# Gate and up projection: a fourth summed K pair, four low weight parts per product made by an accumulating transfer, and matmuls with the low weight part last

## The chip, the core and the metric

The kernel runs on one core of one Trainium2 chip. The metric is device time in microseconds. TensorE (PE) does the matmuls, VectorE (DVE) and ScalarE (ACT) prepare operands and results, GpSimd (POOL) and SyncE (SP) here mostly issue transfers (DMAs); each has its own queue and works it off in order, and they wait for each other by semaphores.

## The reference

An encoder block on 256 tokens of width 2048: two attentions side by side, a cross attention, then a SwiGLU, each added to the residual, and a final norm. What matters here is the SwiGLU with a hidden width of 5632:

```python
hf = rms_norm(x, g_ffn[layer])
x = x + (jax.nn.silu(hf @ w_gate[layer]) * (hf @ w_up[layer])) @ w_down[layer]
return rms_norm(x, g_final)
```

All inputs are float32.

## The kernel before, in words

Every operand of a matmul is split into a high part `h` (the value rounded to the matmul's format) and a low part `l` (what is left), and a product takes three matmuls: high by high, high by low, low by high (`mm`, L97). The activations are the stationary operand (128x128), the weights the moving one (512 columns). ACT makes `wh` by a cast, DVE makes `wl` by subtracting `wh` from the raw weights (`split_into`, L105).

Weights come as "pairs": 256 rows of K by 1024 output columns, 1 MB, in a tile `wraw` with three buffers, loaded by SP (`pair_raw`, L211). `wh` and `wl` have four buffers each, of 1024 columns. A plain pair ("P") is a two by two block product for two token tiles (tt), two column halves (oc) and two K halves (k): 8 products, 24 matmuls. A summed pair ("W") is done with 7 products of sums of blocks (Strassen's scheme in Winograd's form), 21 matmuls: DVE forms four sums of weight blocks `tsum` (L287 to L292, one instruction of 1024 columns and two of 512), and more parts have to be split. The sums of the activations, `forms`, are made once (`summed_pair`, L237).

`wide_project` (L254) goes through the eight pairs of one product in a given order and accumulates in PSUM; `wide_result` (L325) adds what the summed pairs have left, eight instructions of 512 columns on DVE and one copy on ACT. `wide_chunk` (L901) does this for gate, applies Silu on ACT (L906), does the same for up, multiplies and transposes. There are five chunks of 1024 columns, so ten such products, and behind groups of chunks the down projection (`wide_add`, L342) with pairs of its own. `GU_KINDS` (L39) says which pairs are plain or summed, `G_ORDER` and `U_ORDER` (L41) in which order they come; pair i of either is the same slice of the activations.

The order in which each engine gets its instructions is set by a scheduler when the program is built, from the order of the code, buffers and its own estimate of durations. So instructions of neighbouring pairs are interleaved on every engine, but once built the order is fixed.

Of the kernel before, what the change touches and what calls it, by code (L numbers as in the profile page):

```python
# [35 lines left out]
NFC = FF // 512  # L36
NPC = (FF - 512) // 1024

GU_KINDS = "PPWPWPWP"  # L39

G_ORDER, U_ORDER = (0, 1, 2, 3, 4, 5, 6, 7), (0, 2, 1, 4, 3, 6, 5, 7)  # L41

OUT_KINDS, OUT_ORDERS = ("PPPPWWPP", "PPPPWWWP"), ((0, 1, 2, 3, 4, 6, 5, 7), (0, 1, 2, 4, 3, 5, 7, 6))

# [36 lines left out]
def encoder_block(ctx: ExitStack, tc: tile.TileContext, a, out):  # L81
# [14 lines left out]

    def mm(o, l, r, start, stop, seeded=False):  # L97

        nc.tensor.matmul(o, l.h, r.h, start=start, stop=False, skip_group_check=seeded)  # L99
        nc.tensor.matmul(o, l.h, r.l, start=False, stop=False, skip_group_check=seeded)  # L100
        nc.tensor.matmul(o, l.l, r.h, start=False, stop=stop, skip_group_check=seeded)  # L101

    last_split, last_cast = [None], [None]

# [115 lines left out]
        return Split(*[pool.tile([P, 1024], F32R, name=x, tag=x, bufs=bufs)[:, :n * 512].rearrange(  # L220
            "p (b c) -> p b c", b=n) for x in tags])

    def split_blocks(src, pool=None):
        w = w_tile(src.shape[1], pool)
        split_into(w, src)
        return w

    class Pair:
# [22 lines left out]
        split_into(f[:, 4:8, :], s)  # L251
        return Pair(forms=f)

    def wide_project(pairs, src, order, kinds, leave, join, closed=(0, 1), before=None, seed=None):  # L254
# [10 lines left out]
        for n, i in enumerate(order):  # L265
# [2 lines left out]
                before(n)  # L268
            raw = pair_raw(src[i])
            if i not in summed:  # L270
                w = [split_blocks(raw[:, 2 * k:2 * k + 2, :]) for k in range(2)]
                for tt in range(NT):
                    for oc in range(2):
                        for k in range(2):

                            ends = stop or i == plain[-1] and tt == oc == 1
                            mm(accs[tt][oc], pairs[i].at(k, tt), w[k][:, oc, :], not used[tt][oc],
                               ends and k == 1 and oc in closed, seed is not None)
                            used[tt][oc] = True
                continue  # L280
            if i == summed[0]:
                Q = {q: ps_tile(f"q{q}") for q in (1, 5, 7, 6)}
# [24 lines left out]
            own = i == summed[0], i == summed[-1]  # L307
            t1, t3, t2, t4 = [t[:, j, :] for t in (t13, t24) for j in range(2)] if sum_pool else t13 + t24
            A11, A12, A21, A22, S5, S6, S7, S3 = [pairs[i].forms[:, n, :] for n in range(8)]
            mm(Q[1], A11, b11[:, 0, :], *own)  # L310
            mm(accs[0][1], S3, b11[:, 1, :], False, stop, seed is not None)
            mm(Q[5], S5, t1, *own)
            mm(Q[7], S7, t3, *own)
            mm(accs[0][0], A12, b21[:, 0, :], False, stop, seed is not None)
            mm(Q[6], S6, t2, *own)
            mm(accs[1][0], A22, t4, False, stop, seed is not None)
            if i == summed[-1]:
                leave(Q)
        for tt in range(NT):
# [2 lines left out]
        banks.reverse()  # L322
        return accs

    def wide_result(pairs, src, order, kinds):  # L325
# [12 lines left out]
        def join(tt, oc, acc):  # L338
            r = res[tt][:, oc, :]
            nc.vector.tensor_tensor(out=r, in0=acc, in1=r, op=ALU.subtract if (tt, oc) == (1, 0) else ALU.add)  # L340

        wide_project(pairs, src, order, kinds, leave, join)  # L342
        return res

    def wide_add(pairs, src, order, kinds, oc0, done=None, closed=(0, 1), before=None):
# [554 lines left out]

    def wide_chunk(c, kinds):  # L901

        g = wide_result(xn, a["w_gate"][c], G_ORDER, GU_KINDS)
        for tt in range(NT):
            for oc in range(2):
                nc.scalar.activation(g[tt][:, oc, :], g[tt][:, oc, :], AF.Silu)  # L906
        u = wide_result(xn, a["w_up"][c], U_ORDER, GU_KINDS)
# [182 lines left out]
```

## Time and profile before

| | |
|---|---|
| three runs | 1141.78, 1142.07, 1142.09 us (median 1142.07) |
| the profiled execution | 1141.65 us, of which the span from first to last instruction 1139.8 |
| granted clock of TensorE in it | 0.998 |
| DMA | 222.13 MB, mean 195 GB/s |
| queue of the transfers issued by GpSimd | 3.15 MB |

The page gives each engine's busy time and its share of the span, then the chain of work that ended last, then groups of instructions: line, engine, operation, tiles written and read, shape, count, busy us, mean ns of one, and idle time before them with who ended it. A window's row gives the busy us of each engine, the granted clock, the DMA engines' share and GB/s. A row of the timeline gives the start, the length and what ran, with a count where equal instructions are merged. A row of the waits gives who waited for whom: us in total, times, the longest. A DMA row gives the size and the median time from issue to landing.

### The profile page before, as it was taken

What the parts mean: (1) busy time and instruction counts of PE and PEld (TensorE: products, weight loads), DVE (VectorE), ACT (ScalarE), POOL (GpSimd) and SP (SyncE); (2) the same over time, 40 slices, a digit from 0 to 9 for tenths busy, and PEclk for the clock granted to TensorE, in tenths of its full rate; (3) what the DMA queues carried; (4) which work ended last, traced back from release to release, by engine and by line L of the source; (5) the groups of instructions that cost most, each with busy time, mean ns of one, the idle gap of its engine ahead of it and who ended that gap; (6) DMA issues with size and microseconds to landing.
All of it is one profiled execution on the core that took longest, in us unless ns stands there. A gap on an engine that the chain in (4) does not pass through costs nothing.

```text
span 1139.8 us, 14403 instructions
## 1 busy us (share of the span) xinstructions
PE 1130.6 (99%) x5390; PEld 946.4 (83%) x5390; DVE 973.2 (85%) x1322; ACT 667.5 (59%) x965; POOL 58.6 (5%) x75
## 2 busy tenths in 40 slices
PE   9999999999999999999999999999999999999997
PEld 7888888888788888888888888888888888888886
DVE  7788766878896777989898988998998898999895
ACT  7755455567566555665565555565554564665663
POOL 5910000000001000000000000000000000000000
PEclk9999999999999999999999999999999999999999
DMA  9655333546567444455556556556555555565553
GB/s 362 241 195 185 124 125 139 181 149 224 191 227 259 156 161 179 161 211 189 212 194 219 185 191 218 185 190 216 185 187 220 201 205 190 191 247 196 195 181 129
DMA packets 35494, 222.13 MB, mean 195 GB/s; under 512 B 4321, under 2 KB 5601, under 8 KB 11105
## 3 DMA queue, kind: packets, MB, share of 16 engines
q1 hardware_dynamic: 33696, 216.60, 52.9%
q0 software_dynamic: 864, 3.15, 0.8%
q10 hardware_dynamic: 864, 1.47, 0.4%
q8 instruction: 42, 0.69, 0.2%
q14 instruction: 28, 0.22, 0.1%
HBM read 219.11 MB, written 2.10 MB: 194 GB/s over the span
## 4 chain that ended last, share of the span: by engine, by line
PE 98%; issue 1%; ACT 0%; DVE 0%; POOLq 0%; POOL 0%; ACTq 0%
PE acc L99 26%; PE acc L101 26%; PE acc L100 26%; PE q L100 4%; PE q L99 4%; PE q L101 4%; PE pt L502 2%; PE ppt L650 1%; PE psc L100 1%; PE psc L101 1%; PE psc L99 1%; PE acckv L99 0%; PE acckv L101 0%; PE acckv L100 0%; PE pt L922 0%
## 5 line engine op out<-in xcount | busy, mean ns | idle before, releaser
L107 ACT CAST wh<-wraw 128x1024 fp32r<-128x1024 f32 (+2 forms) x401 | 389.8, 989 | 283.2 <-PE acc L101 219.5
L108 DVE TENSOR_TENSOR wl<-wraw,wh 128x1024 fp32r<-128x1024 f32 (+2 forms) x401 | 455.3, 1148 | 88.8 <-ACT wh L107 86.8
L107 ACT CAST wh<-tsum 128x1024 fp32r<-128x1024 f32 (+1 forms) x98 | 98.0, 1006 | 73.1 <-PE acc L101 29.7
L108 DVE TENSOR_TENSOR wl<-tsum,wh 128x1024 fp32r<-128x1024 f32 (+1 forms) x98 | 113.6, 1165 | 19.5 <-ACT wh L107 19.5
L100 PE MATMUL acc<-wl,x2n_h 128*128 128x512 f32 x320 | 124.5, 390 | 0.0
L101 PE MATMUL acc<-wh,x2n_l 128*128 128x512 f32 x320 | 123.9, 389 | 0.0
L99 PE MATMUL acc<-wh,x2n_h 128*128 128x512 f32 x320 | 108.2, 390 | 0.0
L100 PE MATMUL acc<-wl,x0T_h 128*128 128x512 f32 x224 | 88.5, 395 | 0.0
L101 PE MATMUL acc<-wh,x0T_l 128*128 128x512 f32 x224 | 88.2, 394 | 0.0
L99 PE MATMUL acc<-wh,x0T_h 128*128 128x512 f32 x224 | 86.9, 396 | 0.0
L100 PE MATMUL q<-wl,forms_h 128*128 128x512 f32 x191 | 74.3, 389 | 0.0
L101 PE MATMUL q<-wh,forms_l 128*128 128x512 f32 x191 | 74.1, 389 | 0.0
L100 PE MATMUL acc<-wl,hT_h 128*128 128x512 f32 x188 | 73.3, 392 | 0.0
L101 PE MATMUL acc<-wh,hT_l 128*128 128x512 f32 x188 | 72.4, 389 | 0.0
L101 PEld LDWEIGHTS acc<-wh,x2n_l 128*128 128x128 f32 x320 | 60.1, 188 | 12.4
L100 PEld LDWEIGHTS acc<-wl,x2n_h 128*128 128x128 f32 x320 | 60.1, 188 | 12.3
L99 PEld LDWEIGHTS acc<-wh,x2n_h 128*128 128x128 f32 x320 | 59.9, 188 | 12.3
L99 PE MATMUL q<-wh,forms_h 128*128 128x512 f32 x191 | 66.7, 389 | 0.0
L99 PE MATMUL acc<-wh,hT_h 128*128 128x512 f32 x188 | 64.5, 391 | 0.0
L100 PE MATMUL acc<-wl,forms_h 128*128 128x512 f32 x162 | 62.5, 389 | 0.0
L101 PE MATMUL acc<-wh,forms_l 128*128 128x512 f32 x162 | 62.4, 389 | 0.0
L99 PE MATMUL acc<-wh,forms_h 128*128 128x512 f32 x162 | 61.3, 389 | 0.0
(402 smaller groups left out, 2247.9 us busy)
## 6 DMA issues: line engine op xcount, KB each, us to landing
wraw<-in_w_gate SPq DMA_DIRECT2D x44, 1024.0 KB, 4.8
wraw<-in_w_up SPq DMA_DIRECT2D x44, 1024.0 KB, 4.8
wraw<-in_w_dn SPq DMA_DIRECT2D x41, 1024.0 KB, 4.8
wraw<-in_w_in SPq DMA_DIRECT2D x24, 1024.0 KB, 4.8
wraw<-in_w_out SPq DMA_DIRECT2D x16, 1024.0 KB, 4.8
wraw<-in_w_in_lat SPq DMA_DIRECT2D x5, 832.0 KB, 7.2
wraw<-in_w_xk SPq DMA_DIRECT2D x4, 1024.0 KB, 5.4
wraw<-in_w_xq SPq DMA_DIRECT2D x4, 1024.0 KB, 5.9
```

Of the source, the lines that this page charges most:

```text
L99: nc.tensor.matmul(o, l.h, r.h, start=start, stop=False, skip_group_check=seeded)
L100: nc.tensor.matmul(o, l.h, r.l, start=False, stop=False, skip_group_check=seeded)
L101: nc.tensor.matmul(o, l.l, r.h, start=False, stop=stop, skip_group_check=seeded)
L107: last_cast[0] = nc.scalar.copy(out=dst.h, in_=src).ins
L108: last_split[0] = nc.vector.tensor_tensor(out=dst.l, in0=src, in1=dst.h.bitcast(F32), op=ALU.subtract).ins
L502: nc.tensor.transpose(out=pt[:, j * P:(j + 1) * P], in_=src[:, j * P:(j + 1) * P], identity=ident)
L650: nc.tensor.transpose(out=pt[:, kt * S + tt * P:kt * S + (tt + 1) * P], in_=p[:, tt, kt * P:(kt + 1) * P], identity=ident)
```

## The change

Gate and up get four summed pairs of eight in place of three (pair 7 becomes summed), in new orders. In each product four of the 1024-column low parts of plain pairs are made in another way, those in `G_CARRIED` and `U_CARRIED`, as (pair, K half): ACT writes the negated, rounded weights into `wl`, then casts `wh`, and GpSimd issues a transfer of the raw weights (512 KB, from one on-chip tile to another) that adds to what stands in `wl`. DVE has no part in these. In all products of the kernel the matmul with the weights' low part now comes last, and for plain pairs and some summed products, last of several products. The cores of the diff:

```diff
-GU_KINDS = "PPWPWPWP"
-G_ORDER, U_ORDER = (0, 1, 2, 3, 4, 5, 6, 7), (0, 2, 1, 4, 3, 6, 5, 7)
+GU_KINDS = "PPWPWPWW"
+G_CARRIED, U_CARRIED = {(0, 0), (0, 1), (1, 1), (5, 1)}, {(0, 1), (1, 1), (3, 1), (5, 1)}
+G_ORDER, U_ORDER = (0, 1, 2, 4, 3, 6, 7, 5), (0, 2, 1, 4, 3, 6, 7, 5)
...
     def mm(o, l, r, start, stop, seeded=False):
-        nc.tensor.matmul(o, l.h, r.h, start=start, stop=False, skip_group_check=seeded)
-        nc.tensor.matmul(o, l.h, r.l, start=False, stop=False, skip_group_check=seeded)
-        nc.tensor.matmul(o, l.l, r.h, start=False, stop=stop, skip_group_check=seeded)
+        mm_late([(o, l, r, start, stop)], seeded)
+
+    def mm_late(products, seeded=False):
+        for o, l, r, start, stop in products:
+            nc.tensor.matmul(o, l.h, r.h, start=start, stop=False, skip_group_check=seeded)
+            nc.tensor.matmul(o, l.l, r.h, start=False, stop=False, skip_group_check=seeded)
+        for o, l, r, start, stop in products:
+            nc.tensor.matmul(o, l.h, r.l, start=False, stop=stop, skip_group_check=seeded)
...
-    def split_blocks(src, pool=None):
+    def split_blocks(src, pool=None, by_transfer=False):
         w = w_tile(src.shape[1], pool)
-        split_into(w, src)
+        if by_transfer:
+            nc.scalar.activation(w.l, src, AF.Copy, scale=-1.0)
+            last_cast[0] = nc.scalar.copy(out=w.h, in_=src).ins
+            nc.gpsimd.dma_start(out=w.l, in_=src, accum_op=ALU.add)
+        else:
+            split_into(w, src)
         return w
...
-                w = [split_blocks(raw[:, 2 * k:2 * k + 2, :]) for k in range(2)]
-                for tt in range(NT):
-                    for oc in range(2):
-                        for k in range(2):
+                w = [split_blocks(raw[:, 2 * k:2 * k + 2, :], by_transfer=(i, k) in carried) for k in range(2)]
+                for k in range(2):
+                    products = []
+                    for tt in range(NT):
+                        for oc in range(2):
                             ends = stop or i == plain[-1] and tt == oc == 1
-                            mm(accs[tt][oc], pairs[i].at(k, tt), w[k][:, oc, :], not used[tt][oc],
-                               ends and k == 1 and oc in closed, seed is not None)
+                            products.append((accs[tt][oc], pairs[i].at(k, tt), w[k][:, oc, :], not used[tt][oc],
+                                             ends and k == 1 and oc in closed))
                             used[tt][oc] = True
+                    mm_late(products, seed is not None)
...
-            mm(Q[1], A11, b11[:, 0, :], *own)
-            mm(accs[0][1], S3, b11[:, 1, :], False, stop, seed is not None)
-            mm(Q[5], S5, t1, *own)
-            mm(Q[7], S7, t3, *own)
-            mm(accs[0][0], A12, b21[:, 0, :], False, stop, seed is not None)
-            mm(Q[6], S6, t2, *own)
-            mm(accs[1][0], A22, t4, False, stop, seed is not None)
+            mm_late([(Q[1], A11, b11[:, 0, :], *own), (accs[0][1], S3, b11[:, 1, :], False, stop)], seeded)
+            mm_late([(Q[5], S5, t1, *own), (Q[7], S7, t3, *own)], seeded)
+            mm(accs[0][0], A12, b21[:, 0, :], False, stop, seeded)
+            mm_late([(Q[6], S6, t2, *own), (accs[1][0], A22, t4, False, stop)], seeded)
```

The place that is shown now is pair 1 of the up product of the third chunk; the pair that comes before it in the order is pair 2 (summed), the one behind it pair 4 (summed). On ACT before, `wraw_7026` is pair 1, `wraw_6979` pair 2 and `wraw_7060` pair 4; `wh_7028` and `wh_7032` are the two K halves:

```order
L107 CAST wh2_7001<-tsum_6989 128x1024
L107 CAST wh_6995<-wraw_6979 128x512
L107 CAST wh_7028<-wraw_7026 128x1024
L107 CAST wh_7032<-wraw_7026 128x1024
L906 ACTIVATE res1_6893<-res1_6893 128x512 x2
L107 CAST wh_7062<-wraw_7060 128x1024
```

On ACT in the changed kernel, `wraw_7101` is pair 1, `wraw_7054` pair 2 and `wraw_7136` pair 4; `wl_7108` is the carried low part of pair 1's second half:

```order
L115 CAST wh_7070<-wraw_7054 128x512
L919 ACTIVATE res1_6966<-res1_6966 128x512
L115 CAST wh_7103<-wraw_7101 128x1024
L919 ACTIVATE res1_6966<-res1_6966 128x512
L235 CAST wh_7107<-wraw_7101 128x1024
L115 CAST wh_7138<-wraw_7136 128x1024
L234 ACTIVATE wl_7108<-wraw_7101 128x1024
L115 CAST wh_7144<-tsum_7142 128x1024
```

Between the cast of pair 1's first half and the negated copy now stand one Silu and two casts, one of them of the next pair; the transfer is issued by GpSimd behind the copy.

On PE before, at the same pair, where `wl_7029` and `wl_7033` are the low parts that DVE makes:

```order
L100 MATMUL acc_6944<-wl_7029,x2n_h_4508 128x512
L101 MATMUL acc_6944<-wh_7028,x2n_l_4509 128x512
L99 MATMUL acc_6944<-wh_7032,x2n_h_4508 128x512
L99 MATMUL q1_6981<-wh_7062,forms_h_4531 128x512
L100 MATMUL acc_6941<-wl_7033,x2n_h_4508 128x512
L101 MATMUL acc_6941<-wh_7032,x2n_l_4509 128x512
```

On PE in the changed kernel, from the last matmuls with the second half's high part to the first with its carried low part:

```order
L107 MATMUL acc_7018<-wh_7107,x2n_l_4509 128x512
L106 MATMUL q1_7056<-wh_7138,forms_h_4531 128x512
L107 MATMUL q1_7056<-wh_7138,forms_l_4532 128x512
L109 MATMUL q1_7056<-wl_7139,forms_h_4531 128x512
L106 MATMUL q5_7057<-wh_7144,forms_h_4531 128x512
L107 MATMUL q5_7057<-wh_7144,forms_l_4532 128x512
...
L109 MATMUL q7_7058<-wl_7145,forms_h_4531 128x512
L106 MATMUL q6_7059<-wh2_7154,forms_h_4531 128x512
L107 MATMUL q6_7059<-wh2_7154,forms_l_4532 128x512
L109 MATMUL acc_7015<-wl_7108,x2n_h_4508 128x512
```

Eleven matmuls of the next pair now stand ahead of the carried low part. The matmul that frees the buffer for `wh_7103` (the last one with pair 0's first high part) stands 45 matmuls ahead of the first with `wl_7108`.

More of the change, by code (lines that the diff above doesn't have):

```diff
@@ L252, in summed_pair, with wide_project @@
         return Pair(forms=f)
-    def wide_project(pairs, src, order, kinds, leave, join, closed=(0, 1), before=None, seed=None):
+    def wide_project(pairs, src, order, kinds, leave, join, closed=(0, 1), before=None, seed=None, carried=()):
         accs = [[acc_tile() for _ in range(2)] for _ in range(NT)]
@@ L309, in wide_project @@
             A11, A12, A21, A22, S5, S6, S7, S3 = [pairs[i].forms[:, n, :] for n in range(8)]
-            mm(Q[1], A11, b11[:, 0, :], *own)
-            mm(accs[0][1], S3, b11[:, 1, :], False, stop, seed is not None)
-            mm(Q[5], S5, t1, *own)
-            mm(Q[7], S7, t3, *own)
-            mm(accs[0][0], A12, b21[:, 0, :], False, stop, seed is not None)
-            mm(Q[6], S6, t2, *own)
-            mm(accs[1][0], A22, t4, False, stop, seed is not None)
+            seeded = seed is not None
+            mm_late([(Q[1], A11, b11[:, 0, :], *own), (accs[0][1], S3, b11[:, 1, :], False, stop)], seeded)
+            mm_late([(Q[5], S5, t1, *own), (Q[7], S7, t3, *own)], seeded)
+            mm(accs[0][0], A12, b21[:, 0, :], False, stop, seeded)
+            mm_late([(Q[6], S6, t2, *own), (accs[1][0], A22, t4, False, stop)], seeded)
             if i == summed[-1]:
@@ L323, in wide_project, with wide_result @@
         return accs
-    def wide_result(pairs, src, order, kinds):
+    def wide_result(pairs, src, order, kinds, carried):
         res = []
@@ L340, in join @@
             nc.vector.tensor_tensor(out=r, in0=acc, in1=r, op=ALU.subtract if (tt, oc) == (1, 0) else ALU.add)
-        wide_project(pairs, src, order, kinds, leave, join)
+        wide_project(pairs, src, order, kinds, leave, join, carried=carried)
         return res
@@ L901, in wide_chunk @@
     def wide_chunk(c, kinds):
-        g = wide_result(xn, a["w_gate"][c], G_ORDER, GU_KINDS)
+        g = wide_result(xn, a["w_gate"][c], G_ORDER, GU_KINDS, G_CARRIED)
         for tt in range(NT):
@@ L906, in wide_chunk @@
                 nc.scalar.activation(g[tt][:, oc, :], g[tt][:, oc, :], AF.Silu)
[L907 removed]
+        u = wide_result(xn, a["w_up"][c], U_ORDER, GU_KINDS, U_CARRIED)
         t = act_tile(name="hT")
```

## The prediction

> **What bounds the kernel now.** I read the page's engine totals and its chain first, then the windows of the stage that changes, then the timeline of single instructions there, then waits and DMA landings.
>
> ```profile
> PE 1130.6 (99%) x5390; PEld 946.4 (83%) x5390; DVE 973.2 (85%) x1322; ACT 667.5 (59%) x965; POOL 58.6 (5%) x75
> ...
> PE 98%; issue 1%; ACT 0%; DVE 0%; POOLq 0%; POOL 0%; ACTq 0%
> ```
>
> TensorE is busy in 99% of the span and carries 98% of the chain that ended last. The gate and up stage lies in the next window.
>
> ```profile
> 720.00:820.00 100.00, 100.00 (x451) 82.88 (x449) 92.75 (x119) 61.52 (x79) 0.00 (x0) 1.00 0.56 195
> ```
>
> PE has no gap in these 100 us, at a granted clock of 1.00. DVE is busy for 92.75, ACT for 61.52, the DMA engines for 0.56; GpSimd does nothing. So the time is the number of matmuls times their pitch, as long as nobody makes PE wait.
>
> ```profile
> 639.72 0.39 PE L101 MATMUL acc<-wh,forms_l 128*128 128x512 f32 x1
> ...
> 649.92 0.39 PE L101 MATMUL q<-wh,forms_l 128*128 128x512 f32 x1
> ```
>
> The second of these is the 45th matmul after the first: 10.20 / 45 = 0.2267 us apart. Each ends 0.39 after its start.
>
> ```profile
> ACT wh L107 <- PE acc L101: 249.2, 182, 5.4
> DVE wl L108 <- ACT wh L107: 106.3, 136, 3.6
> ```
>
> ACT waits for PE 182 times: the four buffers each of `wh` and `wl` are full, and a cast starts when matmuls free one. DVE waits for ACT. The helpers run as far ahead as the buffers let them; that lead is what the change spends.
>
> **Part 1: matmuls that go.** A plain pair has 8 products of 3 matmuls, a summed one 7. One pair more is summed in each of 5 x 2 products: 10 x 3 = 30 matmuls (the order has 5360 where the page has 5390). 30 x 0.2267 = 6.8 us, all on the path. This is the most that can be won: PE has no other idle time in this stage.
>
> **Part 2: vector and scalar work.** The pitch of each kind is read from runs of equal instructions.
>
> ```profile
> 619.02 3.50 DVE L108 TENSOR_TENSOR wl<-wraw,wh 128x1024 fp32r<-128x1024 f32 x3
> ...
> 1011.26 1.28 DVE L340 TENSOR_TENSOR res<-acc,res 128x512 f32<-128x512 f32 x2
> ```
>
> ```profile
> 617.94 2.95 ACT L107 CAST wh<-wraw 128x1024 fp32r<-128x1024 f32 x3
> ```
>
> ```profile
> L108 DVE TENSOR_TENSOR wl<-wraw,wh 128x1024 fp32r<-128x1024 f32 x334 | 403.9, 1222 | 78.0 <-ACT wh L107 76.3
> L107 ACT CAST wh<-wraw 128x1024 fp32r<-128x1024 f32 x334 | 345.8, 1052 | 238.1 <-PE acc L101 185.4 <-issue 23.7 <-PE q L101 8.7
> ...
> L340 DVE TENSOR_TENSOR res<-acc,res 128x512 f32<-128x512 f32 x40 | 26.3, 682 | 0.4 <-PE acc L101 0.4
> ...
> L906 ACT ACTIVATE res<-res 128x512 f32<-128x512 f32 x20 | 12.3, 629 | 4.6 <-DVE res L340 4.4
> ```
>
> On DVE 1024 columns cost (3.50 - 1.22) / 2 = 1.14 and 512 cost 1.28 - 0.68 = 0.60. A plain pair is two low parts, 2.28. A summed one is four operations of 1024 (three low parts, one sum) and three of 512: 4 x 1.14 + 3 x 0.60 = 6.36. With 8 operations of 512 for the results, a product had 5 x 2.28 + 3 x 6.36 + 4.8 = 35.3 us on DVE against 183 x 0.2267 = 41.5 on PE. Now it has 4 x 2.28 + 4 x 6.36 + 4.8 - 4 x 1.14 = 34.8 against 180 x 0.2267 = 40.8. The carried low parts pay for the added sums; DVE stays at 85% of PE. On ACT a cast of 1024 has a pitch of (2.95 - 1.05) / 2 = 0.95; a product gains 4 negated copies and the casts of one summed pair instead of a plain one (3 x 0.95 + about 0.6 for the one of 512, less 2 x 0.95), about 5.4 us. ACT was 61.52 of 100, so it goes to some three quarters; no time on the path by itself. A negated copy of 1024 is not in the trace; at 512 columns an ACTIVATE takes 629 ns, so between 0.6 and 1.26 for twice that, and I take the cast's 1.05. The extra summed input pair is formed once, beside gate and up of the first 512 columns: below 3 us of DVE, under PE's matmuls. The other reordering (low weight part last, in the whole kernel) gives DVE more time and takes none from PE; where PE had no gap it can only stay equal or open one. I put it at 0, bounds -0.5 and +1.
>
> **Part 3: the 40 transfers, where the answer lies.** A carried low part goes: buffer free, negated copy on ACT, issue on GpSimd, landing, matmul. PE takes its matmuls in order, so a landing after its place in the order stops PE, everything behind it, and through the buffers ACT and DVE. The tightest place is pair 1, second half, of each up product (the rows of the order above). From the last matmul that frees the buffer for its pair's first high part to the first matmul with the carried low part stand 45 matmuls: 45 x 0.2267 = 10.2 us. Off go the matmul's end (0.39), five ACT instructions in front (three casts at 0.95, one ACTIVATE of 512 at 0.60, the copy at 1.05, together 4.50) and 0.15 that I allow for hand-overs. What is left for issue and landing is 5.2 us. The same subtraction for the other parts, five chunks each: gate (0,0) 5.4 to 6.5, (0,1) 7.0 to 8.3, (1,1) 8.6 to 10.8, (5,1) 6.2 to 7.1; up (0,1) 6.1 to 9.1, (1,1) 5.2 in all five, (3,1) 7.5, (5,1) 5.5 twice and 6.2 three times.
>
> How long a landing takes the trace does not show: no transfer in it accumulates. The nearest rows are these; the last two lines are from the two tiles that GpSimd loads, `mn` and `gfb`.
>
> ```profile
> wraw<-in_w_up SPq DMA_DIRECT2D x44, 1024.0 KB, 4.8
> ...
> wraw<-in_w_down SPq DMA_DIRECT2D x6, 512.0 KB, 3.5
> ```
>
> ```profile
> L807 POOL DMA_DIRECT2D mn<-in_mem x4: 537/543/790, 347.5 to 349.4; - x4
> ...
> DMA to landing us min/median/max: 4.9/6.6/10.1
> ```
>
> ```profile
> L952 POOL DMA_DIRECT2D gfb<-in_g_final x2: 527/552/577, 1015.9 to 1016.4; - x2
> ...
> DMA to landing us min/median/max: 6.9/7.2/7.6
> ```
>
> A carried part has the same 512 KB. From below, a copy on SyncE's queue lands in 3.5. From GpSimd the quickest of four took 4.9 and the slower of two 7.6; both groups were issued back to back, so all but the first share the queue. An add also reads what it adds to: twice the bytes on SyncE's queue cost 4.8 - 3.5 = 1.3 more. So 3.5 to 7.6 + 1.3 = 8.9. I take 5.5: nearest to the 4.9 of the first transfer of a group, since carried parts mostly go singly, with half of the second read hidden and both ends in on-chip memory. The Trainium skill, "DMA: Bandwidth & Descriptors", section on the anatomy of a GpSimd DMA, fits 2.0 us plus bytes over 436 GB/s; an estimate from it is 3.2 for 512 KB, nothing would be late, and the time 1135.3. The trace disagrees: 4.9 is its quickest. The page "Collectives: The Full Stack" of the Trainium skill, on why a reduce-scatter runs at half the rate of an all-gather, says an add costs its second source read, which speaks against this change: with it in full, 4.9 + 1.3 = 6.2 us and a time of 1143; no transfer here shows it.
>
> Stalls, part by part: at 5.5, up (1,1) lacks 0.3 five times (1.7), three other places 0.1 each: 2.0 us. At 5.9, some 5. At 6.05, 6.8, and the gain is gone. At 6.2, 8: up (1,1) 1.0 x 5, the last up part 0.7 x 2, the rest 1.6. At 6.9, 18: up (1,1) 1.7 x 5, the last up part 0.7 x 3 and 1.4 x 2, some 4.6 at other parts (a stall gives time to later parts whose buffers were already free; counted once).
>
> What stands behind a waiting instruction: on GpSimd the next carried part; on ACT, behind a copy that waits for its buffer, the casts of the next pair; on SyncE the next load of raw weights, which now waits until the transfer has read its buffer. From the carried part's matmul to the first matmul of the pair loaded into that buffer the order leaves at least 28 matmuls, 6.35 us, against 4.8 for the load and 1.05 for its cast: it fits by 0.5.
>
> **The sum.** The profiled execution took 1141.65 (span 1139.8 and 1.85 around it); the median shown is 1142.07, 0.4 more. -6.8 + 2.0 + 0 = -4.8, on the median 1137.3.
>
> **Rivals.** First, transfers land late: from 6.05 us on the stalls exceed the 6.8 us. For it speak 6.9 to 7.6 at `gfb`, issued in this stage beside a busy DVE and raw loads. Against it, those two shared the queue and came from memory. At 6.9 the time is 1142.07 - 6.8 + 18 = 1153; at 6.2, 1143. Second, two summed pairs in a row starve PE: each needs 6.36 us of DVE in 21 x 0.2267 = 4.76 of PE, 1.6 too much, at 15 places (two in gate, one in up). Half of that exposed at each is 12 us: 1147; it decides once more than 0.45 a place shows. Against it, the sum per product is no larger than before, and low parts are needed later in the pair. Third, transfers land within 5.2: the full 6.8, 1135.3.
>
> **Chances.** A measurement of this kernel tells 0.2%, 2.3 us, from no change. The forecast, landing between 5.2 and 5.8 with a stall under 4.5: 0.35. The third rival: 0.22; together faster 0.57. Late by a little, 5.8 to 6.3: same, 0.14. Later than 6.3: 0.23, and starved by the sums, 0.06: slower 0.29. The range goes from 1135.0, below which I leave 0.03, up to 1150: a landing of 6.7 (15 us of stalls) reaches it, and I leave 0.15 beyond. The faster cases alone are 1135 to 1139.8.
>
> **What would show it.** PE with 5360 matmuls; waits of PE for a DMA `wl<-wraw` short and mostly at up (1,1); the new DMA group near 5.5 us; DVE busy some 5 us less, ACT some 50 more. It is wrong if that group lands after 6 us, if PE waits for DVE `wl` or for ACT, or if loads of `wraw` land much later than 4.8.

## The result and the profile after

The changed kernel takes 1177.87 us (median of four runs, 1176.97 to 1179.23), against 1142.08 for the kernel before on the same chip: a ratio of 1.0315, 95% interval 1.0297 to 1.0332. It is slower by 35.8 us where 4.8 us of gain were forecast, and lies well outside the range.

From the page of the changed kernel, in the order of the page: engine totals, the queues of SyncE's loads and of GpSimd's transfers (packets, MB, their time as a share of 16 engines' span), the chain that ended last, and the new group of transfers.

```profile
PE 1140.5 (97%) x5360; PEld 935.4 (80%) x5360; DVE 974.2 (83%) x1338; ACT 715.7 (61%) x1027; POOL 92.6 (8%) x115
...
q1 hardware_dynamic: 33696, 216.60, 50.2%
q0 software_dynamic: 6624, 24.12, 10.3%
...
PE 74%; DMA 11%; DVE 7%; issue 5%; ACT 2%; SPq 0%; POOLq 0%; POOL 0%; DVEq 0%; ACTq 0%
...
wl<-wraw POOLq DMA_DIRECT2D x40, 512.0 KB, 5.0
```

The 30 matmuls are gone (5360), but PE carries only 74% of the chain, where it carried 98%. DMA stands for 11% of it and DVE for 7%. The waits behind this, in the view of the waits:

```profile
PEld acc L109 <- DMA wl<-wraw: 12.6, 15, 2.1
...
DVE tsum L302 <- DMA wraw<-in_w_up: 12.4, 9, 3.6
DVE tsum L302 <- DMA wraw<-in_w_gate: 11.0, 4, 4.0
...
PEld q L106 <- ACT wh L115: 8.8, 13, 2.0
...
PE acc L109 <- DMA wl<-wraw: 6.9, 8, 1.6
```

There are three kinds (one stall of PE can stand in a row of PEld, the weight loads, and in one of PE): PE waits for carried low parts, PE waits for casts (mostly those of the sums `tsum`), and DVE waits for raw weights of gate and up, 23.4 us in place of 1.5. The median landing, 5.0 us, is below the 5.5 of the forecast. The view of this one tile shows what the median hides (issues with the least, median and greatest length in ns, then the landings in the same way):

```profile
L236 POOL DMA_DIRECT2D wl<-wraw x40: 854/862/936, 471.8 to 1071.3; - x40
...
DMA to landing us min/median/max: 4.5/5.0/9.9
```

What parts the quick from the late is what was issued before them. Of the 40 transfers, 24 were issued when no earlier load or transfer had more than 2.5 us to go: 22 of them landed in 4.5 to 5.0 us, two in 5.1 and 5.8. The other 16 landed in 5.3 to 9.9. One of these shows a transfer that starts later and does not run slower: the one issued at 693.42, behind a load that still took 6.7 us, has its first packet 4.9 us after the issue in place of 1.4, and its packets then take 0.29 us each, where those of a quick one take 0.31. The chain of waits shows such a stretch in the up product of the second chunk (start, length, what; between the lines stand hand-overs and time that the chain does not attribute):

```profile
668.15 4.99 DMA wl<-wraw
...
673.28 6.17 DMA wraw<-in_w_up
...
686.23 4.55 DMA wl<-wraw
...
693.42 9.05 DMA wl<-wraw
...
702.60 6.51 DMA wraw<-in_w_up
...
713.89 4.52 DMA wl<-wraw
...
718.55 8.69 DMA wraw<-in_w_gate
```

Here a load of raw weights starts when a transfer has read its buffer, and lands in 6.2 to 8.7 us in place of 4.8; a transfer of the weights that it brings can only follow behind ACT's work on them, and the next in the chain comes 6.8 us after the first of these loads and 4.8 after the second. Counted over gate and up, 27 of 88 loads took over 5.5 us, 7 of 88 before. So a carried part can be late without a late landing: of the 16 for which PE waits, 7 landed within 5.0 us and had been issued late, with about a quarter of the waiting time.

**Where the time went.** For a table by place, take the distance between the starts of two consecutive matmuls, less 0.2267, where it is positive, and sum it over the matmuls of a weight pair (a matmul is given to its pair by its place in PE's order). This is time by which matmuls came late, in us:

| kernel | gates of the 3rd and 5th chunk | other gates | up | down | sum |
|---|---|---|---|---|---|
| before | 0.7 | 0.4 | 0.2 | 1.2 | 2.5 |
| changed | 17.8 | 3.7 | 10.2 | 11.0 | 42.7 |

The sum grew by 40.2; less the 6.8 us that 30 matmuls took, that is 33.4 of the 35.8 measured. Two of the ten products hold 42% of it. The table serves for the experiments too.

### The profile page after: what moved, and what is told of

It reads as the page before. It is cut to its first block, busy times and chain, and to the rows that moved or that the text cites. A ratio compares the mean times of both kernels' runs of the same rounds, so it can differ in the third digit from the quotient of the medians.

```text
span 1175.5 us, 14852 instructions
## 1 busy us (share of the span) xinstructions
PE 1140.5 (97%) x5360; PEld 935.4 (80%) x5360; DVE 974.2 (83%) x1338; ACT 715.7 (61%) x1027; POOL 92.6 (8%) x115
## 3 DMA queue, kind: packets, MB, share of 16 engines
q1 hardware_dynamic: 33696, 216.60, 50.2%
q0 software_dynamic: 6624, 24.12, 10.3%
## 4 chain that ended last, share of the span: by engine, by line
PE 74%; DMA 11%; DVE 7%; issue 5%; ACT 2%; SPq 0%; POOLq 0%; POOL 0%; DVEq 0%; ACTq 0%
PE acc L106 19%; PE acc L109 19%; PE acc L107 19%; DMA wl<-wraw 6%; DVE wl L116 3%; PE q L106 3%; PE q L107 3%; PE q L109 3%; DMA wraw<-in_w_up 3%; PE pt L515 1%; DVE tsum L302 1%; DMA wraw<-in_w_dn 1%; ACT wh L115 1%; DMA wraw<-in_w_gate 1%; PE ppt L663 1%
## 5 line engine op out<-in xcount | busy, mean ns | idle before, releaser
L116 DVE TENSOR_TENSOR wl<-wraw,wh 128x1024 fp32r<-128x1024 f32 (+2 forms) x361 | 401.7, 1126 | 90.2 <-ACT wh L115 83.4
L115 ACT CAST wh<-wraw 128x1024 fp32r<-128x1024 f32 (+2 forms) x361 | 343.9, 969 | 201.7 <-PE acc L107 144.4
L115 ACT CAST wh<-tsum 128x1024 fp32r<-128x1024 f32 (+1 forms) x118 | 119.2, 1013 | 95.5 <-DVE tsum L302 48.1
L116 DVE TENSOR_TENSOR wl<-tsum,wh 128x1024 fp32r<-128x1024 f32 (+1 forms) x118 | 138.1, 1175 | 12.7 <-ACT wh L115 9.1
L106 PE MATMUL acc<-wh,x2n_h 128*128 128x512 f32 x320 | 125.9, 393 | 4.7 <-DVE res L349 3.0
L109 PE MATMUL acc<-wl,x2n_h 128*128 128x512 f32 x320 | 95.3, 396 | 7.8 <-DMA wl<-wraw 6.9
L106 PE MATMUL q<-wh,forms_h 128*128 128x512 f32 x231 | 92.0, 399 | 8.0 <-ACT wh L115 3.5
L107 PE MATMUL q<-wh,forms_l 128*128 128x512 f32 x231 | 89.9, 390 | 0.0
L302 DVE TENSOR_TENSOR tsum<-wraw 128x1024 f32<-128x1024 f32 x54 | 66.0, 1222 | 27.0 <-DMA wraw<-in_w_up 12.4
L236 POOL DMA_DIRECT2D wl<-wraw x40 | 34.4, 861 | 600.8 <-ACT wl L234 383.5
L109 PEld LDWEIGHTS acc<-wl,x2n_h 128*128 128x128 f32 x320 | 58.6, 188 | 25.9 <-DMA wl<-wraw 12.6
```

What stands on the lines that cost most here:

```text
L107: nc.tensor.matmul(o, l.l, r.h, start=False, stop=False, skip_group_check=seeded)
L109: nc.tensor.matmul(o, l.h, r.l, start=False, stop=stop, skip_group_check=seeded)
L115: last_cast[0] = nc.scalar.copy(out=dst.h, in_=src).ins
L116: last_split[0] = nc.vector.tensor_tensor(out=dst.l, in0=src, in1=dst.h.bitcast(F32), op=ALU.subtract).ins
L236: nc.gpsimd.dma_start(out=w.l, in_=src, accum_op=ALU.add)
L302: nc.vector.tensor_tensor(out=t[:, 0:2, :], in0=raw[:, 1:3, :], in1=raw[:, 0:1, :].to_broadcast([P, 2, 512]), op=ALU.add)
```

## The experiments

**Which part costs.** Four kernels split the change. In the first, nothing is carried:

```diff
-G_CARRIED, U_CARRIED = {(0, 0), (0, 1), (1, 1), (5, 1)}, {(0, 1), (1, 1), (3, 1), (5, 1)}
+G_CARRIED, U_CARRIED = set(), set()
```

> The changed kernel with four summed pairs and low part last, but no low part is carried: DVE makes all. Theory 1 (transfers and loads of raw weights collide on the DMA engines, both land late, PE waits): the waits for DMA go, loads land in 4.8 us again; DVE has 34.8 + 4 x 1.14 = 39.4 us per product against 40.8 of PE, so little lead is left: 1135 to 1145. Theory 2 (two summed pairs in a row starve PE through the sums, the transfers only stand beside): as slow as the change or slower, 1178 and more. Theory 3 (the low part last spoils the order): 1178 too.

1167.15 us, ratio 1.0223 (1.0206 to 1.0240), between the ranges. Without the transfers 10.7 us come back, net of the low parts that DVE now makes itself; 25 stay. In the second, the kinds and orders of before as well, so that only the matmuls' order differs from the kernel before:

```diff
-GU_KINDS = "PPWPWPWW"
+GU_KINDS = "PPWPWPWP"
-G_ORDER, U_ORDER = (0, 1, 2, 4, 3, 6, 7, 5), (0, 2, 1, 4, 3, 6, 7, 5)
+G_ORDER, U_ORDER = (0, 1, 2, 3, 4, 5, 6, 7), (0, 2, 1, 4, 3, 6, 5, 7)
```

> The kernel before with the low weight part last and nothing else: three summed pairs, old orders, no transfers. Theory 1 and theory 2: 1142, within 2. Theory 3: 1160 or more, with idle time of PE in the early stages too.

1148.61 us, ratio 1.0058 (1.0043 to 1.0073), between the ranges again. The reordering alone costs 6.5 us against 1142.08 (6.7 against the 1141.90 of the kernel before on that chip). Its one long wait, in the view of the waits, is at the first down projection, 588 us into the run, for a cast of the activations' sums:

```profile
PEld q L106 <- ACT forms_h L115: 3.4, 1, 3.4
```

Behind it some six matmuls run at half rate (the last section comes to that), so that this one place holds some 4.5 us of the cost.

The third takes the kinds and orders back, but keeps the 40 transfers (same diff, with the carried sets as in the changed kernel):

> The changed kernel with the old three summed pairs and the old orders, and the same 40 carried low parts. DVE then has 35.3 - 4.6 = 30.7 us per product, so the sums cannot starve PE. Theory 1: the collisions stay, loads and transfers land in 6 to 9 us where they meet, 1160 to 1180. Theory 2: 1142, within 3, since DVE has more room than before.

1182.85 us, ratio 1.0360 (1.0344 to 1.0377): 34.2 us above the second, a little more than theory 1 allowed. With three summed pairs the transfers cost nearly what the whole change costs. Its waits:

```profile
ACT wh L115 <- DMA wraw<-in_w_up: 33.1, 14, 4.4
PEld acc L109 <- DMA wl<-wraw: 28.1, 15, 4.3
...
DVE tsum L302 <- DMA wraw<-in_w_up: 25.8, 11, 5.3
...
PE acc L109 <- DMA wl<-wraw: 22.3, 13, 3.8
```

Of its 40.7 us of late matmuls, 31.6 are in up. Here too 15 transfers were issued with less than 2.5 us of earlier ones to go and landed in 4.5 to 5.3 us, the other 25 in 5.0 to 10.1. The fourth kernel is the kernel before with the fourth summed pair and the new orders only (the diff of the second, the other way round):

> The kernel before with the fourth summed pair and the new orders alone: no transfers, and the three matmuls of a product in their old order. If the sums starve PE whatever the order of the matmuls: 1157 to 1167 (1167 of the run without transfers, less the 6.7 that the low part last costs by itself, at most). If the low part last made that starvation: 1135 to 1140.

1170.35 us, ratio 1.0244 (1.0229 to 1.0260), 3 above the first range: 28.3 us lost although 6.8 us of matmuls are gone. Its waits name ACT's casts and, ahead of them, DVE's sums:

```profile
ACT wh L107 <- DVE tsum L287: 46.5, 25, 3.5
...
PEld acc L99 <- ACT wh L107: 13.8, 25, 1.1
...
PEld q L99 <- ACT wh L107: 10.4, 11, 1.6
```

Of its 34.2 us of late matmuls, 18.0 are in the gates of the third and fifth chunk, 3.2 in up. So there are two costs with their weight at different places, 34 and 28 us by themselves. They do not add: from before by way of the reordering (+6.5), the fourth pair (+18.5) and the transfers (+10.7) one comes to the changed kernel's +35.8; by way of the transfers first (+34.2), the fourth pair and its orders then take 5.0 off.

**The transfers: bytes, buffers or place.** A sixteenth of the bytes, first in the changed kernel, then with three summed pairs:

```diff
-            nc.gpsimd.dma_start(out=w.l, in_=src, accum_op=ALU.add)
+            nc.gpsimd.dma_start(out=w.l[:, :, :32], in_=src[:, :, :32], accum_op=ALU.add)
```

> The changed kernel with each of the 40 transfers cut to 32 of every 512 columns, a sixteenth of the bytes; the rest of those low parts stays the negated high part, so that part of the addition is left out. The casts, negated copies, issues and waits all stay. Theory 1 (the bytes of the transfers hold the DMA engines, 2.7 us each at 197 GB/s, and whatever they meet lands late): landings of 3 to 4 us, loads of raw weights back at 4.8, and 1140 to 1150. Theory 4 (the added copies on ACT and the issues on GpSimd are what is late, not the bytes): 1165 or more.

1169.95 us, ratio 1.0244 (1.0229 to 1.0259).

> Three summed pairs in the orders of before, low part last, and 40 transfers cut to 32 of 512 columns each (the rest of the addition is left out, so those low parts are wrong): same copies, issues and waits, a sixteenth of the bytes. Theory B1, the transfers cost by their bytes, which take all 16 DMA engines for 2.7 us and push loads and landings late: close to the kernel without transfers, 1148.6, so 1147 to 1156. Theory B2, they cost by the longer chain of copy, issue and fixed landing, or by the raw buffer held: 1165 to 1183.

1147.34 us, ratio 1.0042 (1.0027 to 1.0057), in B1's range. With three summed pairs nothing of the 34.2 us is left (the kernel without transfers took 1148.61), though it makes the same copies, issues and waits. Its chain, and its landings in the view of the tile:

```profile
PE 97%; issue 1%; DVE 1%; ACT 0%; DMA 0%; POOLq 0%; POOL 0%; SPq 0%; ACTq 0%; DVEq 0%
```

```profile
DMA to landing us min/median/max: 2.5/2.6/6.2
```

So here the bytes are the cost. They act in two ways that this run does not part: the small transfer no longer holds up loads for long, and by itself it lands 2 us sooner (2.5 against 4.5). In the changed kernel 28 us stay when the bytes go, 25 without transfers: that is the other cost, and the run is no evidence for theory 4, in whose range it lies. Two kernels moved or thinned the transfers. Gate's carried parts as up's:

```diff
-G_CARRIED, U_CARRIED = {(0, 0), (0, 1), (1, 1), (5, 1)}, {(0, 1), (1, 1), (3, 1), (5, 1)}
+G_CARRIED, U_CARRIED = {(0, 1), (1, 1), (3, 1), (5, 1)}, {(0, 1), (1, 1), (3, 1), (5, 1)}
```

> The changed kernel with the gate's carried parts moved to the places of up, (0,1), (1,1), (3,1), (5,1): still four per product, but never three within the first two pairs of gate, where landings of 7 to 10 us stand in the trace. Theory 1: the stalls at the gate's start go, some 8 to 15 us of 36: 1163 to 1170. Theory 2: no change, 1178 within 3.

1189.86 us, ratio 1.0423 (1.0404 to 1.0442), worse than either theory said. The late matmuls in the gates fall from 21.5 to 19.3 us, those in up rise from 10.2 to 21.6: the two parts that come together at gate's start are not the main trouble, and moving one of them hurts the product behind. Two carried parts per product, `{(1, 1), (5, 1)}` in both:

> The changed kernel with two carried parts per product, (1,1) and (5,1), which stand apart from each other. DVE has 37.1 us per product of 40.8. Theory 1: half the transfers and none within 5 us of another, so they land near 5 us; the waits for DMA nearly go, those for the sums grow: 1150 to 1162, below both the change and the kernel without transfers. Theory 2 (the sums alone matter): between 1167 and 1178.

1175.14 us, ratio 1.0291 (1.0276 to 1.0306): half the transfers, nearly the same loss (theory 2's range). All but four of the 20 transfers now land within 4.8 us, so DVE, which has two low parts more to make, is likely to have taken back what the transfers gave; no run separates that. A fourth buffer for raw weights, which a transfer could hold without keeping a load waiting:

```diff
-        raw = wp.tile([P, 2048], F32, name="wraw", tag="wraw", bufs=3)
+        turn[0] += 1
+        if sum_pool and turn[0] % 4 == 0:
+            raw = sum_pool[0].tile([P, 2048], F32, name="wraw", tag="wraw2", bufs=1)
+        else:
+            raw = wp.tile([P, 2048], F32, name="wraw", tag="wraw", bufs=3)
...
-    nat_pool[:] = wsum, 5
+    nat_pool[:] = wsum, 4
```

> The changed kernel with a fourth buffer for raw weights from the feed-forward stage on (and four instead of five buffers of the small tiles of 512 columns, to make room). A load then no longer has to wait for the transfer that reads the buffer of three loads ago. Theory 1a (the DMA engines themselves are short when loads and transfers meet): little, 1168 to 1180. Theory 1b (loads start late because the transfer holds the buffer): most of it goes, under 1155.

1170.83 us, ratio 1.0255 (1.0238 to 1.0272). The fourth buffer brings 7.0 us back, net of the small tile given up for it (theory 1a's range); loads over 5.5 us even rose to 38 of 88, and landings reached 11.2. So most of the delay is not the held buffer.

**The fourth pair: neighbours or load.** The forecast's second rival was that two summed pairs in a row starve PE. The first test lets plain and summed pairs alternate, without transfers (against the kernel before):

```diff
-GU_KINDS = "PPWPWPWP"
+GU_KINDS = "PPWPWPWW"
-G_ORDER, U_ORDER = (0, 1, 2, 3, 4, 5, 6, 7), (0, 2, 1, 4, 3, 6, 5, 7)
+G_ORDER, U_ORDER = (0, 2, 1, 4, 3, 6, 5, 7), (0, 2, 1, 4, 3, 6, 5, 7)
```

> The kernel before with the fourth summed pair, as in the earlier run that did this alone, but gate and up both in the order 0 2 1 4 3 6 5 7, so that plain and summed pairs alternate and no two summed ones are neighbours; no transfers, old order of the matmuls. The work on DVE is the same 39.4 us a product (4 x 2.28 + 4 x 6.36 + 4.8) against 180 x 0.2267 = 40.8 of PE. Theory A1, neighbouring summed pairs starve PE: the starved places are gone, 30 matmuls fewer show, 1135 to 1140. Theory A2, DVE's load of 39.4 in 40.8 leaves too little room in any order: 1155 to 1168, with PE still waiting for ACT casts of sums.

1181.67 us, ratio 1.0350 (1.0332 to 1.0367), outside both. The order brought a cost of its own, which its waits show:

```profile
PEld q L99 <- DVE res L340: 10.5, 5, 2.2
...
PE q L99 <- DVE res L340: 8.3, 5, 1.7
...
PEld acc L99 <- DVE res L335: 7.3, 5, 2.8
...
PE acc L99 <- DVE res L335: 5.1, 5, 2.4
```

The last pair is now summed, so that all eight of DVE's instructions that empty accumulators come at a product's end, while the next product wants the accumulators at once. This kernel says nothing on neighbours, and neither does the same order in the changed kernel with its transfers:

> The changed kernel with gate and up in the order 0 2 1 4 3 6 5 7, plain and summed pairs alternating, the 40 transfers kept. Theory A1 with the transfers as a cost of their own: the starved places go, the transfers' loss stays at what it was with three summed pairs (34 us on a kernel without), 1170 to 1182, PE waiting for the DMA of wl. If the two losses are one and the same (transfers only hurt where summed pairs crowd): 1140 to 1155.

1235.80 us, ratio 1.0812 (1.0794 to 1.0830), far above both ranges. Neighbours with three summed pairs, otherwise the kernel before:

```diff
-G_ORDER, U_ORDER = (0, 1, 2, 3, 4, 5, 6, 7), (0, 2, 1, 4, 3, 6, 5, 7)
+G_ORDER, U_ORDER = (0, 1, 2, 4, 3, 5, 6, 7), (0, 1, 2, 4, 3, 5, 6, 7)
```

> The kernel before with its three summed pairs, but gate and up both in the order 0 1 2 4 3 5 6 7, where two summed pairs (2 and 4) are neighbours once in each of ten products; same matmuls, same work on DVE (35.3 us a product). Theory A1: the fourth pair alone lost 28.3 and 6.8 saved, 35 us at 15 neighbouring places, 2.3 each; ten places give 23 us: 1160 to 1168. Theory A2: DVE has room, 1142 to 1146.

1153.16 us, ratio 1.0098 (1.0083 to 1.0113), between the two ranges: 10.9 us. But of its late matmuls 6.1 us are in the two gates, 6.0 in down and only 0.2 in the five up products, which have the same neighbours. Then the fourth pair with gate in up's order, ten neighbouring places in place of fifteen:

```diff
-GU_KINDS = "PPWPWPWP"
+GU_KINDS = "PPWPWPWW"
-G_ORDER, U_ORDER = (0, 1, 2, 3, 4, 5, 6, 7), (0, 2, 1, 4, 3, 6, 5, 7)
+G_ORDER, U_ORDER = (0, 2, 1, 4, 3, 6, 7, 5), (0, 2, 1, 4, 3, 6, 7, 5)
```

> The kernel before with the fourth summed pair and gate in up's order, 0 2 1 4 3 6 7 5: two summed pairs are neighbours once a product, ten places in place of fifteen; the same work on DVE, 39.4 us a product in 40.8 of PE; no transfers, old order of the matmuls. Theory A1, the places are what costs: five fewer at 1.1 (the price measured with three pairs) to 2.3 each, 1158 to 1165. Theory A2, DVE's load is what costs: 1167 to 1172, as with fifteen places (1170.4).

1170.95 us, ratio 1.0253 (1.0237 to 1.0268): as with fifteen, in A2's range. A price per place falls. Next, DVE is relieved by as much as the transfers relieve it, with the changed kernel's orders (in the gates at up's places):

```diff
+        if part:
+            h = wp.tile([P, 1024], F32R, name="wh", tag="wh", bufs=4).rearrange("p (b c) -> p b c", b=2)
+            nc.scalar.copy(out=h, in_=src)
+            return Split(h, h)
...
+w = [split_blocks(raw[:, 2 * k:2 * k + 2, :], part=kinds == GU_KINDS and (i, k) in ((0, 1), (1, 1), (3, 1), (5, 1))) for k in range(2)]
```

> The fourth summed pair in the orders of the changed kernel, without transfers, in the old order of the matmuls, but four low parts a product, of pairs 0, 1, 3 and 5, second half, aren't made at all and their matmuls read the high part a second time (so the products' low parts are left out there): DVE does 34.8 us a product, as the change wanted, with no DMA beside it and no copy on ACT; the same 5360 matmuls. Theory A2, DVE's load: the stalls go and 1135 to 1140 remain. Theory A1, the fifteen places: 1.1 each, 16 us above 1135, so 1148 to 1160.

1156.08 us, ratio 1.0119 (1.0103 to 1.0136). Relief brings 14.3 of the 28.3 back, half. The time lies in A1's range, but A1's price per place had just fallen; A2, which wanted all of it back, is out by 16 us. What is left is at the same places: 10.6 us in the two gates, 9.4 in down, 1.6 in up. A piece of the third chunk's gate, first as PE's timeline (start, length, what, and in brackets the idle time ahead and who ended it), then as a window:

```profile
741.86 0.50 PE L99 MATMUL q<-wh,forms_h 128*128 128x512 f32 x1 [0.62 <-ACT wh L107]
...
746.94 0.50 PE L99 MATMUL q<-wh,forms_h 128*128 128x512 f32 x1 [0.45 <-ACT wh L107]
...
752.19 0.73 PE L99 MATMUL q<-wh,forms_h 128*128 128x512 f32 x2 [0.83 <-ACT wh L107]
```

```profile
741.00:754.00 13.00, 10.65 (x44) 7.54 (x42) 12.67 (x14) 7.77 (x10) 0.00 (x0) 1.00 0.24 81
```

DVE is busy for 12.67 of 13.00 us while PE gets 10.65, and each wait of PE is for a cast of sums that DVE has just made. The relief in plain pairs does not help inside this burst. The same relief with ten neighbouring places:

> The relieved kernel (four low parts a product left out, DVE 34.8 us) with gate in up's order, ten neighbouring places in place of fifteen. Theory A2: 1135 to 1140, as with fifteen. Theory A1: 5.5 us below the relieved kernel with fifteen places, about 1145 to 1153.

1154.72 us, ratio 1.0111 (1.0096 to 1.0126): no different, and outside both ranges. Last, the fourth pair in eight products, without the gates of the third and fifth chunk, and in these two alone (0-based `c`, against the kernel before; the inputs are laid out to match):

```diff
+FOUR, FOUR_ORDERS = "PPWPWPWW", ((0, 1, 2, 4, 3, 6, 7, 5), (0, 2, 1, 4, 3, 6, 7, 5))
+G_FOUR, U_FOUR = (0, 1, 3), (0, 1, 2, 3, 4)
...
-        g = wide_result(xn, a["w_gate"][c], G_ORDER, GU_KINDS)
+        g = wide_result(xn, a["w_gate"][c], *((FOUR_ORDERS[0], FOUR) if c in G_FOUR else (G_ORDER, GU_KINDS)))
...
-        u = wide_result(xn, a["w_up"][c], U_ORDER, GU_KINDS)
+        u = wide_result(xn, a["w_up"][c], *((FOUR_ORDERS[1], FOUR) if c in U_FOUR else (U_ORDER, GU_KINDS)))
```

> The kernel before with the fourth summed pair in eight of the ten products: the gates of the third and fifth chunk keep three, in their old order; no transfers, old order of the matmuls. Theory D, the loss sits where DVE has most besides: in the run with all ten, 18.0 of the late matmuls' 32 us stood in those two gates; without them 14 remain and 24 matmuls fewer (5.4 us) are saved: 1149 to 1153. Rival E, each product with four summed pairs loses alike, 2.83 net: 1142.2 + 8 x 2.83 = 1165.

1159.95 us, ratio 1.0159 (1.0143 to 1.0174). The second has `G_FOUR, U_FOUR = (2, 4), ()`:

> The kernel before with the fourth summed pair in two of the ten products only, the gates of the third and fifth chunk; no transfers, old order of the matmuls. Theory D: 17.4 us more of late matmuls there, less 6 x 0.2267 = 1.4: 1155 to 1160. Rival E: 1142.2 + 2 x 2.83 = 1148.

1153.41 us, ratio 1.0100 (1.0083 to 1.0116). The two losses, 17.7 and 11.2, add up to the 28.3 of all ten within the intervals. A product in the two gates costs 5.6 us, one elsewhere 2.2; the truth lies between the two theories. The first of the two shows how they hang together: with three summed pairs in them, the two gates still hold 8.0 us of late matmuls (0.7 in the kernel before), which points to DVE coming to them late from the up product ahead. In the second they hold 10.8, all their own; with all ten it was 18.0.

**The reordering: inside a product or across.** Only the two low matmuls of each product are exchanged:

```diff
         nc.tensor.matmul(o, l.h, r.h, start=start, stop=False, skip_group_check=seeded)
-        nc.tensor.matmul(o, l.h, r.l, start=False, stop=False, skip_group_check=seeded)
-        nc.tensor.matmul(o, l.l, r.h, start=False, stop=stop, skip_group_check=seeded)
+        nc.tensor.matmul(o, l.l, r.h, start=False, stop=False, skip_group_check=seeded)
+        nc.tensor.matmul(o, l.h, r.l, start=False, stop=stop, skip_group_check=seeded)
```

> The kernel before with one thing changed: inside each product the matmul with the activations' low part comes ahead of the one with the weights' low part, in place of behind it; products stay one after the other, no transfers, three summed pairs. Theory C1, what cost 6.5 us when the low part was put last was putting it last across several products: 1141 to 1143. Theory C2, it is the order inside the product: 1146 to 1150.

1143.59 us, ratio 1.0012 (1.0003 to 1.0021), a little above C1's range. Inside a product the exchange costs 1.4 us; the other 5 come with grouping several products, which in plain pairs also puts all products of one K half ahead of the other. The grouping's late matmuls stand in down: 6.4 us there, 1.2 before.

None of the eighteen kernels beats the kernel before.

## Why the prediction was wrong, step by step

**Part 1, the matmuls that go: right.** 5360 matmuls are left. Their 6.8 us fit the table, where 40.2 us more of late matmuls less 6.8 come near the 35.8 measured, but no kernel with four summed pairs showed them as a gain.

**Part 2, "DVE stays at 85% of PE": the first step that failed.** The sum of 35.3 us counted low parts, sums and results at the pitch of instructions that follow directly on each other, and left out what else DVE does in some products. Windows of the kernel before over two products, from the up product of the second chunk and the gate of the third, have it (us, then busy time of PE, PEld, DVE, ACT, POOL):

```profile
665.00:708.00 43.00, 43.00 (x192) 35.60 (x191) 39.57 (x45) 23.59 (x27) 0.00 (x0) 1.00 0.59 205
709.00:752.00 43.00, 43.00 (x200) 35.68 (x199) 41.09 (x56) 25.63 (x35) 0.00 (x0) 1.00 0.54 191
```

DVE was at 92% in the first and 96% in the second. In the first it does only what the sum counted; the share is higher because an instruction that stands by itself is busy for its whole 1.22 or 0.68 us, not for the pitch of 1.14 or 0.60, and because the window reaches 1.5 us beyond one product. The second is one of the two gates: beside its own work DVE there multiplies the two halves of the chunk before, splits their transposes and makes the sums for the down projection, 20 instructions with 9.4 us of busy time. Taken at some 8 us without their tails, this is an estimate of 35.3 + 8 = 43 us of DVE in the 43.3 that PE's matmuls of such a gate and the transposes among them take: it was full before. A summed pair in place of a plain one adds 6.36 - 2.28 = 4.08 us to DVE and takes 0.68 from PE: 47 in 42.6 in the two gates, 39.4 in 40.8 in an up product. That is where the run with the fourth pair alone lost: 9.0 us of late matmuls in each of the two gates, twice what the estimate lacks, and 0.6 in each up. The forecast had the warning in its own rows (92.75 of 100) and did not set it against its 85%.

That the carried low parts (4.56 a product) pay for the added sums was the next half of that step. In the balance they do; but the run with the same relief and no transfers still lost 13.9 us; the window at 741 us shows why at one place, where the sums come in a burst. That bursts are the reason at the other places too was not shown. ACT was right: the copy measured 1.06 against 1.05 assumed, and ACT is busy for 48 us more. DVE was to be 5 us less busy and is 1.0 more.

**Part 2, the reordering at 0, bounds -0.5 and +1: failed by size.** It is +6.5 alone. The argument "where PE had no gap it can only stay equal or open one" held, and the bound was then set without a row: the place that opened, casts of the activations' sums at the first down projection, was not looked at.

**Part 3, one landing of 5.5 for all: the step that failed among the transfers.** The landing that nothing holds up was even over-estimated (4.5 to 5.0), and the median of 5.0 met the condition of the third rival, whose time of 1135.3 was missed by 42.6 us. What failed is that a landing is one number, and that a load still takes 4.8 beside it ("it fits by 0.5"): 16 of 40 landed in 5.3 to 9.9, 27 of 88 loads took over 5.5, and behind those some carried parts were issued too late. GpSimd's queue shows the reason. On the page of the kernel before it reads:

```profile
q0 software_dynamic: 864, 3.15, 0.8%
```

That is 0.8% of 16 x 1139.8 us, 146 us or 0.17 for each of 864 packets. After, it is 10.3% of 16 x 1175.5 = 1937 us; less those 146, over 5760 packets, 0.31 each. A transfer of 512 KB thus takes 1791 / 40 = 45 us of engine time, all 16 engines for 2.8 us. That is as much as a load of twice its size: q1's 50.2% of the span over 216.60 MB is 46 us for 1 MB. By engine time each product got four loads more to its eight. So transfers and loads push each other back, and a late one holds a buffer that another wants; they queue up, for a load's packet of 8 KB takes 0.36 us before and after. The Trainium skill, "Collectives: The Full Stack", on why a reduce-scatter runs at half the rate of an all-gather, says that an add pays for reading its second source; the packets fit that, at 1.8 times the copy's, though the copies of that queue read from memory and the adding transfers from an on-chip tile. The Trainium skill's page "DMA: Bandwidth & Descriptors", in the section on the anatomy of a GpSimd DMA, gave an estimate of 3.2 us; the quickest landing was 4.5.

**The rivals.** The first, late transfers, was right in direction: PE's weight loads and matmuls wait 12.6 and 6.9 us for carried parts. But its price followed the lead of each part for a common landing, while parts came late that were issued behind a load or transfer with more than 2.5 us to go, or whose own load had been late. The second, sums that starve PE, held 0.06 of the chances and 12 us; alone it is 28.3 net, 35 with the saved matmuls. Its mechanism, DVE slower than PE in a summed pair, is what the window at 741 us shows; its places were wrong: five neighbouring places fewer changed nothing, and with three summed pairs five up products with neighbours held 0.2 us; the products where DVE has least room matter. The two chances were also taken as alternatives, and both came true.

**Open.** Why thinning the transfers to half, or their bytes to a sixteenth, leaves the four-pair kernel no faster than without transfers, although they take 4.56 us a product off DVE (half of it with half the transfers), is not settled: the relief without transfers gave back 14.3 us, in the old order of the matmuls only. Which of the new orders made the step from 1182.85 to 1177.87 was not separated either.

## What to carry to other kernels

Set the work that a change adds to a helper engine against the room that it has in each product's own window, everything else that it does there included, and start with the fullest: an average over products says only that some place has room. A transfer that replaces vector work is paid for in DMA engine time: compare its engine time, not its undelayed landing, with what the loads beside it leave. And where a chain load - transfer - load runs through one ring of buffers, a margin of 0.5 us is none.

## What the hardware showed that was not expected

**Half rate after short stalls.** After some stalls PE runs at half rate for a while. Windows of the alternating kernel (the granted clock stands behind POOL's column):

```profile
526.00:530.00 4.00, 1.60 (x7) 0.98 (x7) 4.00 (x7) 1.71 (x4) 0.00 (x0) 1.00 0.28 119
530.00:534.00 4.00, 4.00 (x12) 3.14 (x11) 4.00 (x6) 1.10 (x2) 0.00 (x0) 0.57 0.30 80
534.00:538.00 4.00, 4.00 (x20) 3.26 (x19) 2.81 (x4) 3.96 (x6) 0.00 (x0) 1.00 0.44 186
```

Its timeline has PE's idle time ahead, and the first slow matmuls:

```profile
527.69 0.50 PE L99 MATMUL q<-wh,forms_h 128*128 128x512 f32 x1 [1.63 <-DVE res L340]
...
529.41 0.50 PE L99 MATMUL acc<-wh,forms_h 128*128 128x512 f32 x1 [0.76 <-ACT wh L107]
...
530.27 0.63 PE L101 MATMUL acc<-wh,x2n_l 128*128 128x512 f32 x1
530.70 0.63 PE L99 MATMUL acc<-wh,x2n_h 128*128 128x512 f32 x1
```

PE was idle for two pieces, 1.63 and 0.76 us, and then some eight matmuls start 0.43 us apart in place of 0.2267. This kernel has seven such stretches with 44 matmuls, some 9 us in all; its granted clock is 0.988. So a stall of 2.4 us here cost 2.4 + 8 x 0.2 = 4.0. The length of one pause does not decide: in the same kernel a lone one of 2.02 us (at 730.70) was followed by such a stretch, while in the kernel with the transfers alone one of 2.80 us (at 1078.87) was not, and the changed kernel, with pauses up to 1.65 us, has none. The Trainium skill, "TensorE: Matmul & The Clock Gate", section "Part 1: The HAM clock gate", puts the drop behind an idle window of about 3.4 us; here it came after pauses of 2.4 us together and after the lone 2.02, so the trace differs there. For the way back the section names sustained work of about 3.4 us; the length of the slow stretch, 8 x 0.43 = 3.4, agrees.

**An adding transfer.** A packet takes 0.31 us where a plain one in the same queue, loading from memory, takes 0.17, and the issue takes GpSimd 0.86 us where a plain one took 0.53 to 0.79.
